# RWKV output product in a hybrid decoder trunk: group-norm statistics, powers, copies and weight splits in another order on VectorE, ScalarE and GpSimd

## The chip, the cores and the metric

The kernel runs on one core of one Trainium2 chip, in float32. The metric is the device time of one execution in microseconds (us). Before the change it is 726.13 us, the median of three runs (725.26 to 726.57). One execution was also recorded by the hardware profiler; every time below that is not a median comes from that record, counted from the start of its span.

## The reference

The program is a decoder trunk of two layers over 256 tokens of width 1024: layer 0 mixes tokens with native sparse attention, layer 1 with RWKV-7, each followed by a squared-ReLU MLP and residual adds. The change touches the end of the RWKV mixer: the states give `y`, which is normalised per head of 64 columns (group norm), gets a bonus, is gated, and goes through the output product into the residual `x`.

```python
    _, ys = lax.scan(step, jnp.zeros((B, H, N, N), f32), xs)
    y = jnp.moveaxis(ys, 0, 1)
    mu = jnp.mean(y, axis=-1, keepdims=True)
    var = jnp.mean(jnp.square(y - mu), axis=-1, keepdims=True)
    yn = ((y - mu) * lax.rsqrt(var + GN_EPS)).reshape(B, S, D) * ln_w + ln_b
    bonus = jnp.sum(rh * kh * r_k.astype(f32).reshape(H, N), axis=-1, keepdims=True) * vh
    y = yn + bonus.reshape(B, S, D)
    return (y.astype(h.dtype) * g) @ w_out, v_first
...
            x = x + y
        x = x + sq_relu_mlp(rms_norm(x, norm_mlp[i]), mlp_w1[i], mlp_w2[i])
```

## The kernel before

**Layout.** The 256 tokens are two tiles of 128 rows, `t = 0` and `t = 1`; a tile of `y` is worked on in two halves of 512 columns (8 heads), `i = 0` and `i = 1`. Names carry both: `rsd10` belongs to tile 1, half 0. The scan runs in four chunks of 64 tokens; chunks 0 and 1 make `y0`, chunks 2 and 3 make `y1`.

**Weights.** Each large weight comes in chunks of 128x1024 by DMA into `wst` (four buffers). ScalarE rounds it to `wh` (line 231), VectorE makes the rest `wl = wst - wh` (line 233, the *split*), and a product is three TensorE matmuls: `wh*h` (267), `wl*h` (268), `wh*l` (269). Below, `wl116` to `wl120` and `rowl` are the splits of six chunks of the output weight. The last two chunks (`row0`, `row1`) stay whole and are multiplied in float32 at line 357.

**Group norm**, `group_norm` at line 1311, for each half: eight `bn_stats` on VectorE (1320), seven small VectorE operations on 128x8 values (1322 to 1328), then on GpSimd a power `rsd = rsd^-0.5` (1329, here *pow*) and a product `nb` (1330). With `rsd` and `nb` ScalarE scales the eight heads (1338; for tile 0, half 1, VectorE does it at 1335). VectorE multiplies by `ln_w`, adds the bonus and gates (1340, 1341, 1342, 128x512 each). TensorE transposes the half into `yTp` (1346). ScalarE copies it out rounded as `yTh` (1349), VectorE makes the rest `yTl` (1350), and of the second half the last two blocks go out whole as `yTf` (1352).

**Output product**, `out_proj` at line 329: TensorE multiplies tile 0 by all chunks into `roa00` and `roa01` (24 three-fold matmuls in the two halves of the weight's columns, then the float32 ones), VectorE adds the result to `x` (378), and `after` transposes `x` for the MLP (`m1p`, 301) and splits it (304, 305). Then tile 1 follows. Between them stand the transposes of tile 1's halves.

**What sets the order.** Each engine runs its instructions strictly in the order of its queue. The queue is made by a scheduler at build time, from the order in which the code issues and from `tc.issue_after(...)`, which keeps an instruction behind another in that order. In `out_proj`, `hold` names instructions behind which the splits of the output weight are issued. At the end of `rwkv` (line 1396 on) the generators of the product and of the norm are advanced alternately. `final` (1414) loads the last norm's weights `gf` with a DMA on GpSimd's queue.

The two places that the change reorders inside `group_norm`:

```python
                    P.tensor_tensor(rsd, rsd, neg_half[:, 0:1].to_broadcast([128, 8]), op=ALU.pow)
                    P.tensor_tensor(nb, bs_, rsd, op=ALU.mult)
...
                    last["yTh"] = act(oh[i][:, :n, sl], p[:, :n], AF.Copy)
                    last["yTl"] = V.tensor_tensor(ol[i][:, :n, sl], p[:, :n], oh[i][:, :n, sl].bitcast(F32), op=ALU.subtract)
                    if i:
                        last["tail"] = act(of[:, :, sl], p[:, 2:], AF.Copy)
```

Of the kernel before, what the change touches and what calls it, by code (L numbers as in the profile page):

```python
# [9 lines left out]
F32 = mybir.dt.float32  # L10
F32R = mybir.dt.float32r
AF = mybir.ActivationFunctionType
ALU = mybir.AluOpType
# [3 lines left out]
D = 1024  # L17
# [5 lines left out]
DH = 64  # L23
# [3 lines left out]
GN_EPS = 64e-5  # L27
# [148 lines left out]
def trunk(ctx: ExitStack, tc: tile.TileContext, wb, x_in, wg, cw1k, cw1v, cw2, vecs_in, l1, w2, a2, g2, rows,  # L176
# [4 lines left out]
    V = nc.vector  # L181
# [103 lines left out]
    last_split, last_tr = [None, None], [None]  # L285

# [588 lines left out]
    def rwkv(inp):  # L875
        hn, dx, xrh, xrl, w2t, a2t, lo = inp
        with ExitStack() as es:
# [433 lines left out]
            def group_norm(t, y_):  # L1311

                for i in range(2):
                    cs = slice(512 * i, 512 * i + 512)
                    hs = slice(8 * i, 8 * i + 8)
                    bst, bs_, rsd, nb = [sm.tile([128, 8] + e, F32, tag=f"{n}", bufs=2, name=f"{n}{t}{i}")
                                         for n, e in (("bst", [6]), ("bs", []), ("rsd", []), ("nb", []))]
                    with tc.issue_after(st_done[1].ins) if t == 0 else ExitStack():
                        for h in range(8):
                            V.bn_stats(bst[:, h], y_[:, (8 * i + h) * DH:(8 * i + h + 1) * DH])  # L1320

                        V.tensor_tensor(nb, bst[:, :, 1], bst[:, :, 4], op=ALU.subtract)
                        V.tensor_tensor(rsd, bst[:, :, 2], bst[:, :, 5], op=ALU.add)
                        V.tensor_tensor(nb, nb, nb, op=ALU.mult)
                        V.tensor_tensor(bs_, bst[:, :, 1], bst[:, :, 4], op=ALU.add)
                        V.scalar_tensor_tensor(rsd, nb, DH / 4.0, rsd, op0=ALU.mult, op1=ALU.add)
                        V.tensor_scalar(bs_, bs_, -0.5, None, op0=ALU.mult)
                        last["stat"] = V.tensor_scalar(rsd, rsd, 1.0 / DH, GN_EPS, op0=ALU.mult, op1=ALU.add)
                    P.tensor_tensor(rsd, rsd, neg_half[:, 0:1].to_broadcast([128, 8]), op=ALU.pow)
                    P.tensor_tensor(nb, bs_, rsd, op=ALU.mult)  # L1330
# [19 lines left out]
                    last["yTl"] = V.tensor_tensor(ol[i][:, :n, sl], p[:, :n], oh[i][:, :n, sl].bitcast(F32), op=ALU.subtract)  # L1350
                    if i:
                        last["tail"] = act(of[:, :, sl], p[:, 2:], AF.Copy)
                    else:
                        last["head"] = last["yTh"], last["yTl"]
# [40 lines left out]
            hl, after = mlp_input(V_GM1, "m1")  # L1395
# [80 lines left out]
```

## Time and profile before

| what | value |
|---|---|
| median of three runs | 726.13 us (725.26 to 726.57) |
| the profiled execution | 725.32 us, of which its span is 723.4 us |
| TensorE (PE) busy | 704.7 us, 97% of the span |
| VectorE (DVE) busy | 466.1 us, 64% |
| ScalarE (ACT) busy | 437.0 us, 60% |
| GpSimd (POOL) busy | 20.9 us, 3% |
| the stretch that the change touches | about 490 to 535 us of the span |

A row of the timeline gives the start, the duration, engine, line, operation, what it writes and reads, how many instructions are merged, and in brackets the idle time of the engine before it with what ended it. Names stand there without buffer numbers. The queues of the engines overlap: a 128x512 VectorE operation is recorded for 0.69 us, while the next independent one starts after 0.60.

### The profile page before, as it was taken

The page shows a single profiled execution, that of the slowest core. Times are in us where ns is not written, and L with a number is a line of the kernel's source. Part 1 is how long each engine was busy: PE and PEld are TensorE (multiplying, and loading weights), DVE is VectorE, ACT ScalarE, POOL GpSimd, SP SyncE. Part 2 cuts the span into 40 slices and gives each one's busy share as a digit, 9 for nine tenths or more (in the row PEclk, how much of TensorE's full clock was granted, in tenths as well). Part 3 has the DMA queues.
Part 4 walks back from the last instruction along what each step waited for, and adds up shares of the span by engine and source line. Part 5 has one row for each costly group of instructions (what it writes and reads, how often), then busy time and mean ns, then how long its engine had stood idle before and what let it go on. Part 6 is the DMA issues. An engine that isn't in the chain of part 4 may idle for free.

```text
span 723.4 us, 13471 instructions
## 1 busy us (share of the span) xinstructions
PE 704.7 (97%) x5290; PEld 600.4 (83%) x5290; DVE 466.1 (64%) x1010; ACT 437.0 (60%) x882; POOL 20.9 (3%) x38
## 2 busy tenths in 40 slices
PE   9999999999999999999999999997999999999996
PEld 7877776789899989998889987686679889998894
DVE  5775899538645445456794879978756455454544
ACT  6735688328655555566275896766557555555552
POOL 1000000000000000000100010002300000000000
PEclk9999999999999999999999999999999999999998
DMA  7947020125755555578015432143428555555521
GB/s 286 318 168 292 25 93 2 59 88 207 235 180 195 180 181 196 177 228 268 1 59 175 137 109 63 31 148 102 163 78 267 183 196 181 188 189 177 195 95 58
DMA packets 32156, 111.64 MB, mean 154 GB/s; under 512 B 3677, under 2 KB 4189, under 8 KB 32094
## 3 DMA queue, kind: packets, MB, share of 16 engines
q1 hardware_dynamic: 31022, 109.08, 44.7%
q10 hardware_dynamic: 928, 1.19, 0.7%
q8 instruction: 41, 0.67, 0.4%
q0 software_dynamic: 144, 0.52, 0.2%
q14 instruction: 21, 0.17, 0.1%
HBM read 108.69 MB, written 1.05 MB: 152 GB/s over the span
## 4 chain that ended last, share of the span: by engine, by line
PE 83%; DVE 9%; ACT 4%; issue 2%; DMA 1%; SPq 0%; POOLq 0%; POOL 0%; DVEq 0%; ACTq 0%
PE mu L267 9%; PE mu L268 8%; PE mu L269 8%; PE mo L267 8%; PE mo L269 8%; PE mo L268 8%; PE acc L268 2%; PE acc L269 2%; PE acc L267 2%; PE S L654 2%; PE pa L268 2%; PE pa L267 2%; PE pa L269 2%; DVE pd L1201 2%; DVE Tb L1204 1%
## 5 line engine op out<-in xcount | busy, mean ns | idle before, releaser
L233 DVE TENSOR_TENSOR wl<-wst,wh 128x1024 fp32r<-128x1024 f32 x175 | 213.7, 1224 | 172.4 <-ACT wh L231 171.8
L231 ACT ACTIVATE wh<-wst 128x1024 fp32r<-128x1024 f32 x175 | 184.9, 1061 | 158.0 <-PE mu L268 77.5
L267 PE MATMUL mo<-wh,mqh 128*128 128x512 f32 x224 | 88.6, 397 | 0.0
L268 PE MATMUL mo<-wl,mqh 128*128 128x512 f32 x224 | 88.4, 395 | 0.0
L269 PE MATMUL mo<-wh,mql 128*128 128x512 f32 x224 | 87.4, 396 | 0.0
L267 PE MATMUL mu<-m0h,wh 128*128 128x256 f32 x256 | 72.5, 285 | 0.4 <-DVE m0l L305 0.4
L269 PE MATMUL mu<-m0h,wl 128*128 128x256 f32 x256 | 72.3, 283 | 0.0
L268 PE MATMUL mu<-m1l,wh 128*128 128x256 f32 x256 | 72.0, 282 | 0.0
L268 PE MATMUL mu<-m0l,wh 128*128 128x256 f32 x256 | 71.8, 282 | 0.0
L269 PE MATMUL mu<-m1h,wl 128*128 128x256 f32 x256 | 71.7, 281 | 0.0
L267 PE MATMUL mu<-m1h,wh 128*128 128x256 f32 x256 | 71.3, 282 | 0.0
L269 PEld LDWEIGHTS mo<-wh,mql 128*128 128x128 f32 x224 | 42.1, 188 | 10.3
L267 PEld LDWEIGHTS mu<-m0h,wh 128*128 128x128 f32 x256 | 48.2, 189 | 1.8 <-DVE m0l L305 0.6
L268 PEld LDWEIGHTS mu<-m0l,wh 128*128 128x128 f32 x256 | 48.4, 189 | 1.3 <-DVE m0l L305 0.2
L268 PEld LDWEIGHTS mu<-m1l,wh 128*128 128x128 f32 x256 | 48.2, 188 | 1.2
L267 PEld LDWEIGHTS mu<-m1h,wh 128*128 128x128 f32 x256 | 47.8, 188 | 1.2
L268 PEld LDWEIGHTS mo<-wl,mqh 128*128 128x128 f32 x224 | 42.2, 188 | 8.0
L267 PEld LDWEIGHTS mo<-wh,mqh 128*128 128x128 f32 x224 | 42.1, 188 | 7.7
L269 PEld LDWEIGHTS mu<-m1h,wl 128*128 128x128 f32 x256 | 48.2, 188 | 0.0
L269 PEld LDWEIGHTS mu<-m0h,wl 128*128 128x128 f32 x256 | 48.1, 188 | 0.0
L267 PE MATMUL acc<-wh,n0h 128*128 128x512 f32 x80 | 31.9, 405 | 0.1
L268 PE MATMUL acc<-wl,n0h 128*128 128x512 f32 x80 | 31.3, 397 | 0.2 <-DVE wl L233 0.2
(378 smaller groups left out, 1429.7 us busy)
## 6 DMA issues: line engine op xcount, KB each, us to landing
wst<-in_wb_dram SPq DMA_DIRECT2D x186, 512.0 KB, 4.1
w1t<-in_cw1k_dram SPq DMA_DIRECT2D x4, 512.0 KB, 6.1
w1t<-in_cw1v_dram SPq DMA_DIRECT2D x4, 512.0 KB, 7.0
x<-in_x_dram SPq DMA_DIRECT2D x4, 256.0 KB, 4.9
VS<-vt ACTq DMA_DIRECT2D x8, 128.0 KB, 4.6
row<-in_wb_dram SPq DMA_DIRECT2D x2, 512.0 KB, 4.7
out_dram<-xg SPq DMA_DIRECT2D x4, 256.0 KB, 2.1
g<-in_l_dram SPq DMA_DIRECT2D x2, 320.0 KB, 5.8
```

What stands on the lines that cost most here:

```text
L231: act(wh, st, AF.Copy)
L233: wl_done.append(V.tensor_tensor(wl, st, wh.bitcast(F32), op=ALU.subtract))
L267: mm(o, lh, rh, start=first, stop=False)
L268: mm(o, lh, rl, start=False, stop=False)
L269: return mm(o, ll, rh, start=False, stop=last)
L654: mm(S1, qT[gp][:, hg, 128:256], kT[gp][:, s], start=True, stop=True)
L1201: V.tensor_tensor(pd[:, a, :m_], Tb[:, a, i][:, :, None].to_broadcast(sh), Lb[:, i, n:][:, None, :].to_broadcast(sh), op=ALU.mult)
L1204: V.tensor_tensor(Tb[:, a, n:], Tb[:, a, n:], pd[:, a, :m_], op=ALU.add)
```

## The change

It sets the order of the norm's work by hand. The statistics of a half become a function, `gn_stats`, with their own places in the order: for tile 1, half 0, they come behind the `yTl` of tile 0, half 0; for tile 1, half 1, behind the split that is fourth in the output product (`wl119`). On GpSimd the product `nb` of one half comes ahead of the power of the next. `yTf` is copied ahead of `yTl`. The holds of the splits name other instructions, and the load of `gf` comes behind the last `nb`.

```diff
+            def gn_stats(t, i, y_):
+
+                bst, bs_, rsd, nb = [sm.tile([128, 8] + e, F32, tag=f"{n}", bufs=2, name=f"{n}{t}{i}")
+                                     for n, e in (("bst", [6]), ("bs", []), ("rsd", []), ("nb", []))]
+                with tc.issue_after((last["wl3"] if i else last["head"][1]) .ins if t else st_done[1].ins):
+                    for h in range(8):
+                        V.bn_stats(bst[:, h], y_[:, (8 * i + h) * DH:(8 * i + h + 1) * DH])
...
+                with tc.issue_after(last["nb"].ins) if i else ExitStack():
+                    P.tensor_tensor(rsd, rsd, neg_half[:, 0:1].to_broadcast([128, 8]), op=ALU.pow)
+                last["nb"] = pool_last[0] = P.tensor_tensor(nb, bs_, rsd, op=ALU.mult)
+                return rsd, nb
...
-                    last["yTl"] = V.tensor_tensor(ol[i][:, :n, sl], p[:, :n], oh[i][:, :n, sl].bitcast(F32), op=ALU.subtract)
                     if i:
                         last["tail"] = act(of[:, :, sl], p[:, 2:], AF.Copy)
-                    else:
+                    last["yTl"] = V.tensor_tensor(ol[i][:, :n, sl], p[:, :n], oh[i][:, :n, sl].bitcast(F32), op=ALU.subtract)
+                    if not i and not t:
                         last["head"] = last["yTh"], last["yTl"]
...
+            stat0 = last["stat"]
+            first_half = gn_stats(1, 0, y[1])
+            n_wl = len(wl_done)
             out = out_proj(lambda k, sl: kt(oh, k)[:, sl], lambda k, sl: kt(ol, k)[:, sl], "ro", after, tail=8, own=3,
-                           hold=[(last["stat"].ins, last["VS", 1].ins)] * 2 + [(last["o"].ins, last["VS", 3].ins)]
-                           + [[i_.ins for i_ in last["head"]] + [last["yc"].ins]], whole=of, marks=last)
+                           hold=[(stat0.ins, last["VS", 1].ins)] * 2 + [(last["head"][1].ins, last["VS", 3].ins)]
+                           + [[last["head"][0].ins, last["stat"].ins, last["yc"].ins]], whole=of, marks=last)
             next(out)
             done(AR, Wt)
             next(out)
-            norm = group_norm(1, y[1])
+            last["wl3"] = wl_done[n_wl + 3]
+            norm = group_norm(1, y[1], first_half)
...
-        P.dma_start(gf, bass.AP(tensor=rows.tensor, offset=rows.offset, ap=[[0, 128], [1, D]]))
+        with tc.issue_after(pool_last[0].ins):
+            P.dma_start(gf, bass.AP(tensor=rows.tensor, offset=rows.offset, ap=[[0, 128], [1, D]]))
```

The small statistics operations and the scaling loop are the same code as before, moved. Line numbers behind line 285 grow, by 2 in the helpers and by 7 to 12 in the places below.

GpSimd's queue, the four powers (`rsd` with `neg_half`) and products (`nb`), before, from the second power on:

```order
L1329 TENSOR_TENSOR rsd01_5750<-rsd01_5750,neg_half_71 128x8
L1330 TENSOR_TENSOR nb00_5676<-bs00_5674,rsd00_5675 128x8
L1330 TENSOR_TENSOR nb01_5751<-bs01_5749,rsd01_5750 128x8
L1329 TENSOR_TENSOR rsd10_5886<-rsd10_5886,neg_half_71 128x8
L1416 DMA gf_7819<-in_rows_dram 128x1024
L1330 TENSOR_TENSOR nb10_5887<-bs10_5885,rsd10_5886 128x8
L1329 TENSOR_TENSOR rsd11_5943<-rsd11_5943,neg_half_71 128x8
```

Now, from the first product on:

```order
L1330 TENSOR_TENSOR nb00_5676<-bs00_5674,rsd00_5675 128x8
L1329 TENSOR_TENSOR rsd01_5750<-rsd01_5750,neg_half_71 128x8
L1330 TENSOR_TENSOR nb01_5751<-bs01_5749,rsd01_5750 128x8
L1329 TENSOR_TENSOR rsd10_5794<-rsd10_5794,neg_half_71 128x8
L1330 TENSOR_TENSOR nb10_5795<-bs10_5793,rsd10_5794 128x8
L1329 TENSOR_TENSOR rsd11_5943<-rsd11_5943,neg_half_71 128x8
L1330 TENSOR_TENSOR nb11_5944<-bs11_5942,rsd11_5943 128x8
L1428 DMA gf_7819<-in_rows_dram 128x1024
```

`nb00` moved ahead of the power of `rsd01`, and the load of `gf` from between `rsd10` and `nb10` to the end.

VectorE's queue behind the last gating of `y0`, before:

```order
L233 TENSOR_TENSOR wl118_5822<-wst118_5818,wh118_5820 128x1024
L1320 BN_STATS bst10_5884<-y1_5636 128x6 x8
L1322 TENSOR_TENSOR nb10_5887<-bst10_5884 128x8
L1323 TENSOR_TENSOR rsd10_5886<-bst10_5884 128x8
L1325 TENSOR_TENSOR bs10_5885<-bst10_5884 128x8
L1324 TENSOR_TENSOR nb10_5887<-nb10_5887 128x8
L1327 TENSOR_SCALAR bs10_5885<-bs10_5885 128x8
L1350 TENSOR_TENSOR yTl0_5489<-yTp_5705,yTh0_5487 128x4x128
L1326 SCALAR_TENSOR_TENSOR rsd10_5886<-nb10_5887,rsd10_5886 128x8
L1328 TENSOR_SCALAR rsd10_5886<-rsd10_5886 128x8
L1320 BN_STATS bst11_5941<-y1_5636 128x6 x8
L1322 TENSOR_TENSOR nb11_5944<-bst11_5941 128x8
```

Now, from the same place:

```order
L1359 TENSOR_TENSOR yTl0_5489<-yTp_5705,yTh0_5487 128x4x128
L1319 BN_STATS bst10_5792<-y1_5636 128x6 x8
L233 TENSOR_TENSOR wl118_5843<-wst118_5839,wh118_5841 128x1024
L1321 TENSOR_TENSOR nb10_5795<-bst10_5792 128x8
L1322 TENSOR_TENSOR rsd10_5794<-bst10_5792 128x8
L1324 TENSOR_TENSOR bs10_5793<-bst10_5792 128x8
L1323 TENSOR_TENSOR nb10_5795<-nb10_5795 128x8
L1326 TENSOR_SCALAR bs10_5793<-bs10_5793 128x8
L1325 SCALAR_TENSOR_TENSOR rsd10_5794<-nb10_5795,rsd10_5794 128x8
L1327 TENSOR_SCALAR rsd10_5794<-rsd10_5794 128x8
L233 TENSOR_TENSOR wl119_5855<-wst119_5851,wh119_5853 128x1024
L1319 BN_STATS bst11_5941<-y1_5636 128x6 x8
```

`yTl0` moved to the front, and directly behind the last operation on `rsd10` stands a split, `wl119`, where before the eight statistics of the next half stood.

VectorE's queue further on, before:

```order
L233 TENSOR_TENSOR wl119_5834<-wst119_5830,wh119_5832 128x1024
L1323 TENSOR_TENSOR rsd11_5943<-bst11_5941 128x8
L1325 TENSOR_TENSOR bs11_5942<-bst11_5941 128x8
L1324 TENSOR_TENSOR nb11_5944<-nb11_5944 128x8
L233 TENSOR_TENSOR wl120_5846<-wst120_5842,wh120_5844 128x1024
L1327 TENSOR_SCALAR bs11_5942<-bs11_5942 128x8
L1326 SCALAR_TENSOR_TENSOR rsd11_5943<-nb11_5944,rsd11_5943 128x8
L233 TENSOR_TENSOR rowl_5858<-wst121_5854,rowh_5856 128x1024
L1350 TENSOR_TENSOR yTl1_5490<-yTp_5780,yTh1_5488 128x2x128
L1328 TENSOR_SCALAR rsd11_5943<-rsd11_5943 128x8
L1340 TENSOR_TENSOR y1_5636<-y1_5636,lnw_5365 128x512
```

Now, from the split of chunk 120 on:

```order
L233 TENSOR_TENSOR wl120_5867<-wst120_5863,wh120_5865 128x1024
L233 TENSOR_TENSOR rowl_5879<-wst121_5875,rowh_5877 128x1024
L1321 TENSOR_TENSOR nb11_5944<-bst11_5941 128x8
L1359 TENSOR_TENSOR yTl1_5490<-yTp_5780,yTh1_5488 128x2x128
L1322 TENSOR_TENSOR rsd11_5943<-bst11_5941 128x8
L1324 TENSOR_TENSOR bs11_5942<-bst11_5941 128x8
L1323 TENSOR_TENSOR nb11_5944<-nb11_5944 128x8
L1347 TENSOR_TENSOR y1_5636<-y1_5636,lnw_5365 128x512
L1326 TENSOR_SCALAR bs11_5942<-bs11_5942 128x8
L1325 SCALAR_TENSOR_TENSOR rsd11_5943<-nb11_5944,rsd11_5943 128x8
L1348 TENSOR_TENSOR y1_5636<-y1_5636,vt1_4609 128x512
L1327 TENSOR_SCALAR rsd11_5943<-rsd11_5943 128x8
```

The last operation on `rsd11`, which the fourth power reads, moved from ahead of the `ln_w` multiplication of tile 1, half 0, to behind that and behind the bonus addition (1348 now).

On TensorE one thing moves: the four `m1p` transposes of the second half of `x`'s columns, tile 0, from between the matmuls of tile 1 to directly behind those of the first half, ahead of the `yTp` transposes of tile 1, half 1.

## Rows read from the trace of the kernel before

**Rows 1.** From the page: its first line, and the shares of the chain that ended last.

```profile
span 723.4 us, 13471 instructions
...
PE 83%; DVE 9%; ACT 4%; issue 2%; DMA 1%; SPq 0%; POOLq 0%; POOL 0%; DVEq 0%; ACTq 0%
```

**Rows 2.** Timeline of TensorE: start, duration, line, out<-in, count, [idle before <- releaser].

```profile
495.82 0.68 PE L1261 MATMUL pZ<-W,AR 64*64 64x64 f32 x28
497.72 1.15 PE L1271 MATMUL pQ<-Zt,TT 64*64 64x64 f32 x32 [1.22 <-ACT Zt L1263]
...
501.63 0.66 PE L1346 MATMUL yTp<-cst,y 128*128 128x128 f32 x4 [0.26 <-DVE y L1342]
...
506.28 0.50 PE L267 MATMUL roa<-wh,yTh 128*128 128x512 f32 x1 [1.71 <-DVE yTl L1350]
...
512.91 0.40 PE L269 MATMUL roa<-wh,yTl 128*128 128x512 f32 x1
...
517.26 0.63 PE L1346 MATMUL yTp<-cst,y 128*128 128x128 f32 x4 [0.60 <-DVE y L1342]
...
520.87 0.63 PE L1346 MATMUL yTp<-cst,y 128*128 128x128 f32 x4 [0.82 <-DVE y L1342]
```

**Rows 3.** The chain that ended last, in order of time: the second `m1p` group.

```profile
525.93 0.44 PE m1p L301 x4
```

**Rows 4.** Timeline of GpSimd: powers (L1329) and products (L1330) of the norm.

```profile
491.93 2.36 POOL L1329 TENSOR_TENSOR rsd<-rsd,neg_half 128x8 f32<-128x8 f32 x1
494.26 0.20 POOL L1330 TENSOR_TENSOR nb<-bs,rsd 128x8 f32<-128x8 f32 x1
...
506.68 1.64 POOL L1329 TENSOR_TENSOR rsd<-rsd,neg_half 128x8 f32<-128x8 f32 x1 [11.79 <-ACT wh L231]
...
509.06 1.24 POOL L1330 TENSOR_TENSOR nb<-bs,rsd 128x8 f32<-128x8 f32 x1
...
513.77 0.20 POOL L1330 TENSOR_TENSOR nb<-bs,rsd 128x8 f32<-128x8 f32 x1
```

**Rows 5.** Timeline of VectorE: splits (L233), statistics, gating, last operation on `rsd11`.

```profile
491.56 2.35 DVE L233 TENSOR_TENSOR wl<-wst,wh 128x1024 fp32r<-128x1024 f32 x2
...
502.21 0.69 DVE L1342 TENSOR_TENSOR y<-y,g 128x512 f32<-128x512 f32 x1
...
506.41 1.11 DVE L1320 BATCH_NORM_STATS2 bst<-y 128x6 f32<-128x64 f32 x8
...
507.64 1.22 DVE L233 TENSOR_TENSOR wl<-wst,wh 128x1024 fp32r<-128x1024 f32 x1
...
509.03 1.21 DVE L233 TENSOR_TENSOR wl<-wst,wh 128x1024 fp32r<-128x1024 f32 x1
...
511.79 0.16 DVE L1328 TENSOR_SCALAR rsd<-rsd 128x8 f32<-128x8 f32 x1
```

**Rows 6.** Timeline of ScalarE: copies of the state, scalings (L1338), the copy of `yTf`.

```profile
491.99 1.59 ACT L1274 ACTIVATE VS<-pQ 64x256 f32<-64x256 f32 x4 [0.49 <-PE pQ L1271]
494.49 2.76 ACT L1338 ACTIVATE y<-y,nb,rsd 128x64 f32<-128x64 f32 x8 [0.91 <-POOL nb L1330]
...
511.91 0.39 ACT L1352 ACTIVATE yTf<-yTp 128x256 f32<-128x256 f32 x1 [4.12 <-DVE yTl L1350]
512.19 5.41 ACT L1338 ACTIVATE y<-y,nb,rsd 128x64 f32<-128x64 f32 x16
```

**Rows 7.** Stretches at the span's end: length, busy time of each engine, granted clock, DMA.

```profile
718.00:719.00 1.00, 0.00 (x0) 0.00 (x0) 0.33 (x2) 0.17 (x1) 0.56 (x1) 1.00 0.00 0
719.00:720.00 1.00, 0.00 (x0) 0.00 (x0) 0.31 (x1) 0.55 (x1) 0.00 (x0) 0.55 0.00 0
```

**Rows 8.** Timeline of TensorE: its last matmul.

```profile
715.91 0.40 PE L269 MATMUL mo<-twh,mql 128*128 128x512 f32 x1
```

**Rows 9.** Timeline of TensorE at the span's start, the warm-up matmuls.

```profile
1.05 3.79 PE L477 MATMUL warmp<-warmz 128*128 128x128 f32 x16 [1.05 <-DVE warmz L472]
...
6.11 1.50 PE L477 MATMUL warmp<-warmz 128*128 128x128 f32 x12
```

More of the change, by code (lines that the diff above doesn't have):

```diff
@@ L285, in trunk @@
     last_split, last_tr = [None, None], [None]
+    pool_last = [None]
     def after_split():
@@ L1309, in output @@
                     done(Ms[c], VS[c])
-            def group_norm(t, y_):
+            def gn_stats(t, i, y_):
[4 more added lines that the diff above has]
+                        V.bn_stats(bst[:, h], y_[:, (8 * i + h) * DH:(8 * i + h + 1) * DH])
+                    V.tensor_tensor(nb, bst[:, :, 1], bst[:, :, 4], op=ALU.subtract)
+                    V.tensor_tensor(rsd, bst[:, :, 2], bst[:, :, 5], op=ALU.add)
+                    V.tensor_tensor(nb, nb, nb, op=ALU.mult)
+                    V.tensor_tensor(bs_, bst[:, :, 1], bst[:, :, 4], op=ALU.add)
+                    V.scalar_tensor_tensor(rsd, nb, DH / 4.0, rsd, op0=ALU.mult, op1=ALU.add)
+                    V.tensor_scalar(bs_, bs_, -0.5, None, op0=ALU.mult)
+                    last["stat"] = V.tensor_scalar(rsd, rsd, 1.0 / DH, GN_EPS, op0=ALU.mult, op1=ALU.add)
+                with tc.issue_after(last["nb"].ins) if i else ExitStack():
+                    P.tensor_tensor(rsd, rsd, neg_half[:, 0:1].to_broadcast([128, 8]), op=ALU.pow)
+                last["nb"] = pool_last[0] = P.tensor_tensor(nb, bs_, rsd, op=ALU.mult)
+                return rsd, nb
@@ L1313, in group_norm @@
+            def group_norm(t, y_, first_half=None):
                 for i in range(2):
                     cs = slice(512 * i, 512 * i + 512)
[L1315 to L1328, printed above, removed]
@@ L1329, in group_norm @@
-                    P.tensor_tensor(rsd, rsd, neg_half[:, 0:1].to_broadcast([128, 8]), op=ALU.pow)
-                    P.tensor_tensor(nb, bs_, rsd, op=ALU.mult)
+                    rsd, nb = first_half if first_half and not i else gn_stats(t, i, y_)
                     with tc.issue_after(st_done[2].ins) if t == 0 and i else ExitStack():
```

## The prediction, made before the changed kernel ran

> **What bounds the kernel now.** I read the page first: of the chain that ended last, 83% is TensorE's, so time is saved or lost only where TensorE waits, or where it is given other work [rows 1]. Then TensorE's timeline between 490 and 535, for its waits: 1.22 us until `Zt` is copied, 0.26 for the first `yTp`, 1.71 until VectorE has made `yTl0`, 0.60 and 0.82 for the gated halves of `y1` [rows 2]. They sum to 4.6 us, 0.6% of the span, and no order can give back more. Last come the engines that are waited for: VectorE's queue [rows 5], ScalarE's scalings [rows 6], and GpSimd's powers [rows 4], which look idle (3% busy) but stand in the middle of each norm.
>
> **The change part by part.** Times are on the scale of the profiled execution. Terms 2 to 4 are worked out as if all ahead of 502 stayed where it is; term 1 then moves the whole of it.
>
> *Term 1, `nb00` ahead of the second power.* Now `nb00` starts at 494.26, after the second power (491.93, 2.36 us), and ScalarE idles 0.91 us for it before the first scalings [rows 4, 6]. Changed, `nb00` is issued at 492.0, when the first power ends. It then stands beside the two splits of 491.56 [rows 5]. What a GpSimd operation does that starts inside a split is in the rows: `nb10` started at 509.06, 0.03 after a split, and lasted 1.24 us, to 0.06 after the split's end, where `nb11`, beside nothing, took 0.20; and the second power, started inside the first of the two splits, lasted 0.7 longer than the third (1.64) and came through between the two [rows 4, 5]. So it is held until the split in progress ends. `nb00` ends at 492.8, ScalarE is free at 491.99 + 1.59 = 493.6, the scalings run 493.6 to 496.35 instead of 494.49 to 497.25 [rows 6]. TensorE has `pZ` done at 496.50, so `Zt` and `pQ` come 0.7 earlier and VectorE's gating of `y0` 0.9 earlier; the first `yTp`, which had 0.26 of waiting on top, moves from 501.63 by 0.9 [rows 2]. Were `nb00` held over both splits (to 494.0), it would be 0.5. I take **-0.9**, since the row next to it slipped through.
>
> *Term 2, `yTl0` first.* VectorE ends its gating at 502.9 [rows 5]. Now 118's split and the statistics come before `yTl0`, and TensorE waits 1.71. Changed: `yTl0` 502.95; eight statistics 503.55 (1.11 recorded, the next may start after 1.03); `wl118` 504.6 (1.14 from start to start: two take 2.35); seven small operations from 505.7 to 506.5; `wl119` 506.45; eight statistics 507.6; `wl120` 508.6; `rowl` 509.75; one small; `yTl1` 511.0 to 511.4. TensorE starts the product 1.7 earlier, and meets `rowl` and `yTl1` at its 28th and 29th matmul. The 29th, now at 512.91, goes at 511.45: of 1.7 us 1.45 is left. From there to the next `yTp` is 517.26 - 512.91 - 0.60 = 3.75 us of work, so that could stand at 515.2 instead of 517.26 [rows 2].
>
> *Term 3, powers behind splits.* This is where the change pays. Before, the power of `rsd10` started at 506.68 beside the statistics and took 1.64 unhindered [rows 4, 5]. Changed, `wl119` follows `rsd10` at once, so the power starts 0.2 after a split has begun: held to 507.55, done 509.2. `nb10` then starts inside `wl120` and ends with it, at 509.9. ScalarE, no longer stopped 4.12 us by `yTf` behind `yTl1` [rows 6], waits for this instead: eight scalings of 0.34, 509.95 to 512.65. VectorE, there at 511.57, multiplies by `ln_w` from 512.7, adds at 513.5, and only then does the last operation on `rsd11`, 514.1 to 514.3, that ended at 511.95 before [rows 5]. The fourth power starts inside the gating of 514.25 to 514.95, is done at 516.45, `nb11` at 516.7 (before: 513.97 [rows 4]), the scalings at 519.45, where they ended at 512.19 + 5.41 = 517.60 [rows 6]. The five VectorE operations from there to the second gating are the same in number and sum, so the second `yTp` of tile 1, at 520.87 now, comes at 522.7: **+1.8**. The gain of term 2 runs out here: it only makes TensorE wait longer. The gating of 514.95 is still in time for the `yTp` of 515.2.
>
> *Term 4, `m1p`.* The second group of four transposes took 0.44 us between tile 1's matmuls [rows 3]; now it fills a wait: **-0.45**.
>
> *Costed at nothing.* `gf` is needed only in the last MLP, 170 us later. The DMA that refills 118's buffer goes out 1.7 later than at 504, for a rounding behind 522. The new semaphore waits of ScalarE's scalings are for statistics long done.
>
> The sum is -0.9 + 1.8 - 0.45 = **+0.45 us**.
>
> *Term 5, TensorE's clock.* TensorE's first `m1p` group ends at 515.2 + (520.87 - 0.82 - 517.26) = 518.0, and the next work, for which VectorE adds to `x` behind the delayed scalings, starts at 522.05: one wait of 4.1 us in place of several short ones. In the whole trace TensorE's longest wait between its first and last matmul is the 1.71 of [rows 2], with the granted clock at 1.00. Behind its last matmul, over at 716.3 [rows 8], the clock is 1.00 until 719 and then falls to half, 1.2 GHz: the mean of 0.55 puts the fall at 719.1, 2.8 us later [rows 7]. A wait of 4.1 us lies beyond that, so I expect the lower level when tile 1's matmuls begin. What it costs no row shows in mid-run. Below it is nothing, if the clock recovers at once. Above: the first 16 warm-up matmuls took 0.237 us each, those at 6.11 0.125 [rows 9]; half speed from 1.05 to about 6 loses 2.4 us. I take the middle, **+1.2**, since the end of the low stretch may fall anywhere.
>
> The Trainium skill, "TensorE: Matmul & The Clock Gate", section "HAM oscillation — how this bites in real kernels", tells of a kernel whose waits for data let the clock fall to half, so that each next burst of matmuls starts slow; by that rule the wait speaks against this change. The fall after the last matmul agrees [rows 7]; that a wait in mid-run does it, no row here shows.
>
> The Trainium skill, "SBUF — State Buffer", section "Who interferes with whom", says that the engine that comes first, GpSimd or a VectorE operation with two inputs in SBUF, holds the shared ports for its whole instruction. The half that holds GpSimd agrees with [rows 4, 5]. The other half does not: the split of 507.64 began inside the power of 506.68 to 508.32 and took its usual 1.22 [rows 5]. By the rule the split of 508.6 would wait for the power's end at 509.2; the rival below has what follows.
>
> **The rivals.**
> 1. *GpSimd is held, the clock stays up.* 726.13 + 0.45 = 726.6. For it: how long a wait the chip bears in mid-run is not in the trace, and where the fall came may have been late. This is the nearest case on the other side.
> 2. *GpSimd isn't held.* Then the third power runs 506.65 to 508.3, `nb10` is ready at 508.5, VectorE goes on at 511.57 without waiting, `rsd11` is ready 1.1 earlier, the fourth power ends at 514.95, the scalings at 517.9, 0.3 later than before. Sum 0.3 - 0.45 - 0.9 = -1.05: 725.1, the most that I see in the change. Against it: every power or product that began beside a split in [rows 4] was stretched.
> 3. *GpSimd is held longer.* `nb10` doesn't come through between `wl120` and `rowl`, which stand back to back, and ends with `rowl` at 511.05: 1.1 more, 726.13 + 0.45 + 1.1 + 1.2 = 728.9. It decides from a gap that is too short; the second power found one.
> 4. *A power in progress stops a split.* `wl120` at 509.2 makes `nb10` 0.5 later: 0.95 + 1.2, 728.3. The row above speaks against it.
>
> That the change doesn't do what it says isn't open: the queues stand as built.
>
> **How the numbers follow.** The profiled execution took 725.32, 0.8 below the median; the terms are differences, and I add them to the median. Forecast (held, clock falls): 726.13 + 0.45 + 1.2 = **727.8**, chance 0.45, by itself 726.6 to 729.0 for a price of the clock of 0 to 2.4. Rival 1 0.25, rival 2 0.17, rivals 3 and 4 0.08 together, anything else 0.05. About 0.2%, 1.45 us, is what a measurement of this kernel can tell from no change: slower is above 727.6, faster below 724.7. In the forecast the price decides: above 1.0 of 0 to 2.4 it is slower, 0.26 of its 0.45; with rivals 3 and 4 and some of the rest 0.36. Rival 1 and the other part of the forecast and most of rival 2 are the same: 0.55. Faster is the lower end of rival 2 and some of the rest: 0.09. The range of 8 in 10 takes in rivals 1 to 4 with half a microsecond below rival 2: 724.6 to 729.2.
>
> **What would show it.** Right: the first scalings start 0.9 earlier and TensorE's wait for `pQ` shrinks to about 0.5; no wait ahead of the first `roa` matmul; the power of `rsd10` lasts about 2.5 us and `nb10` about 0.6; VectorE idles over 1 us ahead of tile 1's first `ln_w`; TensorE has one wait of about 4 us ahead of the second `m1p`; and behind it a stretch with a granted clock below 1.00 and matmuls of twice the length. Wrong: a third power of 1.64 us beside `wl119` (term 3 falls, rival 2), or the 4 us wait at a clock that stays at 1.00 (term 5 falls, rival 1).

## The result, and the profile after

The changed kernel took 730.41 us (median of five runs, 728.52 to 731.5), the kernel before 725.54 beside it (724.5 to 726.57): a ratio of 1.0056, with a 95% interval of 1.0038 to 1.0075. The middle of the forecast was 1.7 us slower, though the prediction gave 0.55 to no measurable change and 0.36 to slower. It is slower, by 4.9 us, and outside of the range.

The profiled execution of the changed kernel has a span of 728.5 us, 5.1 more than [rows 1]. Since the two executions differ ahead of the change too, I measure by a stretch that holds only the change and the work behind it: from the start of GpSimd's first power to the start of the last matmul. Before: 715.91 - 490.31 = 225.60 us [rows 8]. After: 720.36 - 491.16 = 229.20. So 3.60 of the 5.1 us lie there; 0.85 came ahead of it, and 0.65 behind the last matmul.

TensorE's timeline of the changed kernel (start, duration, line, out<-in, count, [idle before <- releaser]):

```profile
497.87 1.15 PE L1273 MATMUL pQ<-Zt,TT 64*64 64x64 f32 x32 [0.53 <-ACT Zt L1265]
...
504.29 0.48 PE L267 MATMUL roa<-wh,yTh 128*128 128x512 f32 x1
...
516.12 0.63 PE L1353 MATMUL yTp<-cst,y 128*128 128x128 f32 x4 [0.88 <-DVE y L1349]
516.59 1.88 PE L359 MATMUL roa<-row,yTf 128*128 128x512 f32 x4
518.31 0.60 PE L303 MATMUL m1p<-cst,x 128*128 128x128 f32 x4
523.12 1.11 PE L303 MATMUL m1p<-cst,x 128*128 128x128 f32 x4 [4.21 <-DVE x L380]
...
526.59 0.63 PE L268 MATMUL roa<-wl,yTh 128*128 128x512 f32 x1
527.02 0.63 PE L269 MATMUL roa<-wh,yTl 128*128 128x512 f32 x1
...
528.12 0.39 PE L269 MATMUL roa<-wh,yTl 128*128 128x512 f32 x1
528.35 0.40 PE L267 MATMUL roa<-wh,yTh 128*128 128x512 f32 x1
```

Of the waits of [rows 2], the one for `Zt` is 0.53 instead of 1.22, the one ahead of the first `roa` matmul is gone, and the one for the gated first half of `y1` is 0.88 instead of 0.60. A new one of 4.21 us stands ahead of the second `m1p` group, for VectorE's addition to `x`. Behind it a matmul follows the one before after 0.43 us; from 528 on it is 0.23 again. The granted clock of the same stretch (length, busy time of PE, PEld, DVE, ACT and POOL, granted clock, DMA):

```profile
520.00:521.00 1.00, 0.00 (x0) 0.00 (x0) 0.42 (x1) 1.00 (x4) 0.00 (x0) 1.00 1.04 377
521.00:522.00 1.00, 0.00 (x0) 0.00 (x0) 1.00 (x3) 0.28 (x2) 0.00 (x0) 0.52 0.25 86
...
526.00:527.00 1.00, 1.00 (x3) 0.73 (x3) 0.76 (x3) 0.30 (x2) 0.00 (x0) 0.50 0.00 0
527.00:528.00 1.00, 1.00 (x4) 0.78 (x3) 0.00 (x0) 0.31 (x1) 0.00 (x0) 0.57 0.00 0
528.00:529.00 1.00, 1.00 (x6) 0.81 (x5) 0.22 (x1) 1.00 (x3) 0.00 (x0) 1.00 0.00 0
```

The clock falls to half (1.2 GHz) at 521.0, 2.1 us after TensorE's last work, and comes back at 527.9, 4.7 us after the next work began. (In the second profile of this kernel, below, it falls at 521.4 and comes back at 528.2: 2.5 us and 5.1 us.) Where the 4.21 us come from, GpSimd shows (`nb00`, the second power, the third, `nb10`, the fourth, `nb11`):

```profile
492.88 0.80 POOL L1330 TENSOR_TENSOR nb<-bs,rsd 128x8 f32<-128x8 f32 x1
493.65 2.62 POOL L1329 TENSOR_TENSOR rsd<-rsd,neg_half 128x8 f32<-128x8 f32 x1
...
506.62 2.48 POOL L1329 TENSOR_TENSOR rsd<-rsd,neg_half 128x8 f32<-128x8 f32 x1 [9.96 <-ACT wh L231]
509.19 1.79 POOL L1330 TENSOR_TENSOR nb<-bs,rsd 128x8 f32<-128x8 f32 x1
515.41 2.06 POOL L1329 TENSOR_TENSOR rsd<-rsd,neg_half 128x8 f32<-128x8 f32 x1 [4.44 <-DVE rsd L1327]
517.55 0.20 POOL L1330 TENSOR_TENSOR nb<-bs,rsd 128x8 f32<-128x8 f32 x1
```

and VectorE beside it (`wl119`, `wl120`, `rowl`, the first `ln_w` of tile 1, the last operation on `rsd11`, the second `ln_w`, the second addition to `x`):

```profile
506.39 1.23 DVE L233 TENSOR_TENSOR wl<-wst,wh 128x1024 fp32r<-128x1024 f32 x1
...
508.55 1.21 DVE L233 TENSOR_TENSOR wl<-wst,wh 128x1024 fp32r<-128x1024 f32 x1
509.68 1.22 DVE L233 TENSOR_TENSOR rowl<-wst,rowh 128x1024 fp32r<-128x1024 f32 x1
...
513.81 0.69 DVE L1347 TENSOR_TENSOR y<-y,lnw 128x512 f32<-128x512 f32 x1 [2.23 <-ACT y L1345]
...
515.17 0.17 DVE L1327 TENSOR_SCALAR rsd<-rsd 128x8 f32<-128x8 f32 x1
...
520.58 0.69 DVE L1347 TENSOR_TENSOR y<-y,lnw 128x512 f32<-128x512 f32 x1 [4.00 <-ACT y L1345]
...
522.39 0.68 DVE L380 TENSOR_TENSOR x<-x,roa 128x512 f32<-128x512 f32 x1
```

and ScalarE with tile 1's scalings, which wait for `nb10` and for `nb11`:

```profile
511.01 2.77 ACT L1345 ACTIVATE y<-y,nb,rsd 128x64 f32<-128x64 f32 x8 [2.99 <-POOL nb L1330]
517.78 2.76 ACT L1345 ACTIVATE y<-y,nb,rsd 128x64 f32<-128x64 f32 x8 [4.01 <-POOL nb L1330]
```

Read together: the third power stretched by `wl119`, `nb10` held not to the end of `wl120` (509.76) but to that of `rowl` (510.90); the scalings of half 0 therefore late, VectorE waiting 2.23 us; the last operation on `rsd11`, queued behind, at 515.17 instead of 511.79 [rows 5]; the fourth power behind it; and a wait of 4.00 us on VectorE, which passes on to TensorE. VectorE's queue has a part in that last step: the matmuls that the second addition to `x` reads end at 518.47 (516.59 + 1.88), but the addition stands behind the `ln_w` multiplication that waits, and comes at 522.39. No run here puts it ahead of that multiplication.

### The profile page after: what moved, and what is told of

Same layout as the page of the kernel before. It is cut to its first block, busy times and chain, and to the rows that moved or that the text cites. A ratio compares the mean times of both kernels' runs of the same rounds, so it can differ in the third digit from the quotient of the medians.

```text
span 728.5 us, 13474 instructions
## 1 busy us (share of the span) xinstructions
PE 707.1 (97%) x5290; PEld 602.1 (83%) x5290; DVE 465.5 (64%) x1010; ACT 436.6 (60%) x882; POOL 23.5 (3%) x38
## 4 chain that ended last, share of the span: by engine, by line
PE 83%; DVE 9%; ACT 4%; issue 2%; DMA 1%; POOL 0%; SPq 0%; POOLq 0%; DVEq 0%
PE mu L267 8%; PE mu L268 8%; PE mu L269 8%; PE mo L267 8%; PE mo L269 8%; PE mo L268 8%; PE acc L268 2%; PE acc L269 2%; PE acc L267 2%; PE S L656 2%; PE pa L268 2%; PE pa L267 2%; PE pa L269 2%; DVE pd L1203 2%; DVE Tb L1206 1%
## 5 line engine op out<-in xcount | busy, mean ns | idle before, releaser
L233 DVE TENSOR_TENSOR wl<-wst,wh 128x1024 fp32r<-128x1024 f32 x175 | 213.6, 1224 | 173.7 <-ACT wh L231 173.1
```

The source lines that it names most:

```text
L233: wl_done.append(V.tensor_tensor(wl, st, wh.bitcast(F32), op=ALU.subtract))
```

## The experiments

In this table "stretch" is the one from the first power's start to the last matmul, of the profiled execution; the ratio is to the kernel before in the same set of runs.

| kernel | stretch, us | ratio (95%) |
|---|---|---|
| before; again | 225.60; 225.67 | 1 |
| changed; again | 229.20; 229.37 | 1.0056 (1.0038 to 1.0075); 1.0067 (1.0050 to 1.0084) |
| before, `nb00` ahead | 224.70 | 0.9995 (0.9984 to 1.0007) |
| changed, 28 needless matmuls | 228.94 | 1.0048 (1.0034 to 1.0063) |
| changed, 16 needless matmuls | 227.35 | 1.0050 (1.0034 to 1.0066) |
| changed, `rsd11` ahead of `ln_w` | 223.59 | 0.9976 (0.9963 to 0.9989) |
| changed, `rsd11` ahead of `ln_w`, `nb10` on VectorE | 223.69 | 0.9980 (0.9964 to 0.9996) |
| changed, statistics ahead of `wl119` | 222.76 | 0.9948 (0.9931 to 0.9966) |
| changed, `rowl` last | 223.65 | 0.9983 (0.9971 to 0.9995) |
| changed, `wl119` in the statistics | 222.31 | 0.9954 (0.9935 to 0.9973) |

**The two kernels again.** The changed kernel a second time:

> The changed kernel once more, beside the kernel before on the same chip. Its profile began the norm's stretch 0.85 us later than the kernel before (TensorE waited 1.35 instead of 0.81 us at 471 and 0.63 instead of 0.36 at 477), at code that the change does not touch. Theory A, that this belongs to one execution: the two waits come back at other lengths, and the ratio is 1.004 to 1.007 all the same. Rival, that it belongs to the changed program: 1.35 and 0.63 come back to 0.05 us. In both cases the product of GpSimd for tile 1, half 0, should again last about 1.8 us, if being held through two splits is not chance.

The kernel before a second time:

> The kernel before, profiled a second time, for the stretch ahead of the norm, in which five profiles of changed kernels began the first power at 490.7 to 491.6 us, and the profile of the kernel before at 490.3. Theory A, TensorE's waits at 471 and 477 us (0.81 and 0.36 us in the kernel before, 1.15 to 1.35 and under 0.2 to 0.91 in the others) have lengths of chance, which belong to one execution: here they differ from 0.81 and 0.36 too, by up to 1 us in the start of the first power. Rival, they belong to the changed program: 0.81, 0.36 and 490.3 come back to 0.1 us.

In the changed kernel every row of the norm came back, `nb10` with 1.80 us and TensorE's wait with 4.21. The rows ahead of it came back too, or nearly: waits of 1.25 and 0.63 us (1.35 and 0.63 in the first profile), the first power at 491.18 (491.16). By that run alone, the rival would stand. The kernel before, though, began its first power at 492.59 this time, 2.28 us later than in its first execution, with a longer wait of TensorE and a clock that fell to half in the middle of the scan. Its rows, from TensorE's timeline, then those of the first execution:

```profile
471.93 1.15 PE L1257 MATMUL pZ<-VS,M 128*64 128x64 f32 x32 [1.83 <-DVE TT L1232]
473.01 1.94 PE L1183 MATMUL pKB<-cst,BK 128*128 128x128 f32 x8
```

```profile
470.57 1.15 PE L1257 MATMUL pZ<-VS,M 128*64 128x64 f32 x32 [0.81 <-DVE TT L1232]
471.65 1.09 PE L1183 MATMUL pKB<-cst,BK 128*128 128x128 f32 x8
```

The second row took 1.09 us there, where the clock stayed up. So the start of the norm moves by more than 0.85 us between two executions of one kernel; and in the six profiles of the changed kernel and its variants in which the clock did not fall ahead of the norm, it lies between 490.71 and 491.61. The 0.85 us are no more than such differences; that no part of them belongs to the change is not shown.

**Term 1 alone.** Kernel before, with

```diff
-                    P.tensor_tensor(rsd, rsd, neg_half[:, 0:1].to_broadcast([128, 8]), op=ALU.pow)
-                    P.tensor_tensor(nb, bs_, rsd, op=ALU.mult)
+                    with tc.issue_after(last["nb"].ins) if t == 0 and i else ExitStack():
+                        P.tensor_tensor(rsd, rsd, neg_half[:, 0:1].to_broadcast([128, 8]), op=ALU.pow)
+                    last["nb"] = P.tensor_tensor(nb, bs_, rsd, op=ALU.mult)
```

> The kernel before with one part of the change: the product nb00 ahead of the second power on GpSimd's queue, nothing else. Theory A, term 1 of the prediction by itself: nb00 lasts 0.8 us and ends with the first split, the scalings follow ScalarE's copies without their 0.91 us of waiting, and 0.9 us come off: ratio to the kernel before 0.9988. Rival, nothing of it is left at the first tile-1 matmul, since the order behind it (the split of 118 and the statistics ahead of yTl0) sets the time: the wait ahead of the first roa matmul grows from 1.71 to 2.6, ratio 1.000.

`nb00` lasted 0.80 us again, and the stretch is 0.90 to 0.97 shorter. The wait ahead of the first `roa` matmul stays at 1.70, so the rival, by which it would grow to 2.6, falls. The timing, -0.05% with an interval of -0.16 to +0.07%, holds both 0.9 us and nothing; the stretch decides.

**What the clock costs.** In the changed kernel, ahead of tile 0's second `m1p` group,

```diff
+            if (name, t, cbs) == ("m1", 0, (1,)):
+                for j in range(28):
+                    mm(p[:, j % 4], ident, ident, start=True, stop=True)
```

> The changed kernel with 28 needless 128x128 matmuls between the two m1p groups of tile 0, which fill TensorE's wait of 4.2 us (28 x 0.125 = 3.5 us at full clock) and are overwritten. Nothing else moves ahead of the wait. Theory A, the wait costs twice, once as waiting and once as clock: the granted clock stays at 1.00 between 519 and 530, the first seven threefold matmuls of tile 1 start 0.23 us apart instead of 0.43, and the kernel is 2.2 us faster than the changed one, ratio to the kernel before about 1.003 (728.0 where the changed one has 730.2). Rival, the lower clock is only a bystander and the matmuls are slow for their operands: no gain, ratio 1.006.

Here my sizing was off: the trace has two instructions for each of these matmuls, and the 56 took 6.42 us, so that the second `m1p` group started 1.9 us later than in the changed kernel, counted from the first power. The clock stayed at 1.00, and the stretch is 0.26 us shorter all the same; the ratio, 1.0048, can't be told from the changed kernel's. The same with `range(16)`:

> The changed kernel with 16 needless matmuls in TensorE's wait in place of the 28 of the run before, in which each was two instructions and the 56 took 6.42 us, 1.9 us longer than the wait. 16 take 3.7 us and fit into it. Theory A, the clock has a price of 2.2 us by itself: the granted clock stays 1.00, the second m1p group starts where it did in the changed kernel, counted from the first, the next matmuls start 0.23 us apart, ratio to the kernel before 1.003 (changed: 1.0056 and 1.0067). Rival, a shorter wait than in the changed kernel is what the run before gained by: no gain, 1.006.

TensorE's timeline in this kernel:

```profile
523.83 0.66 PE L306 MATMUL m1p<-cst,x 128*128 128x128 f32 x4 [0.64 <-DVE x L383]
...
525.22 0.39 PE L268 MATMUL roa<-wl,yTh 128*128 128x512 f32 x1
525.45 0.39 PE L269 MATMUL roa<-wh,yTl 128*128 128x512 f32 x1
```

The second group starts 31.96 us after the first power, as in the changed kernel (523.12 - 491.16 = 31.96), so nothing moved ahead of it, and behind it the clock is what differs, 1.00 here. The stretch is 1.85 us shorter than in the changed kernel's first profile, and 2.02 than in its second, where the clock came back 0.4 us later. That is the price of the clock by these three profiles: 1.9, not the expected 2.2. The timing (1.0050, where 1.003 was expected) cannot confirm it; its interval holds the changed kernel's ratio as well.

**The late `rsd11`.** Changed kernel; the statistics of half 1 are issued from within the product, with no other place, and

```diff
...
-                    with tc.issue_after((wl_done[-1] if t else st_done[2]).ins):
+                    with tc.issue_after((wl_done[-1] if t else st_done[2]).ins), tc.issue_after(last["stat"].ins) if t else ExitStack():
                         V.tensor_tensor(y_[:, cs], y_[:, cs], lnw[0][:, cs], op=ALU.mult)
...
```

> The changed kernel with one group moved on VectorE: the last three operations on bs11 and rsd11 stand ahead of the ln_w multiplication of tile 1, half 0, as in the kernel before. Theory A, the late rsd11 is what turns a short hold into a long wait: the fourth power starts at 511.9 and runs beside nothing (1.64 us), the second half's scalings follow the first half's without a gap (513.8 to 516.5 instead of 517.8 to 520.5), TensorE's wait ahead of the second m1p shrinks from 4.2 to about 0.5 us, the clock stays at 1.00, and of the 4.9 us lost 6.4 come back: 0.997 of the kernel before. Rival, GpSimd's hold of the third power and product (506.6 to 511.0) is what costs, whatever follows: the wait stays above 2 us, and the ratio above 1.002.

GpSimd's fourth power and product, then TensorE:

```profile
511.61 1.64 POOL L1332 TENSOR_TENSOR rsd<-rsd,neg_half 128x8 f32<-128x8 f32 x1 [1.08 <-DVE rsd L1330]
513.33 0.20 POOL L1333 TENSOR_TENSOR nb<-bs,rsd 128x8 f32<-128x8 f32 x1
```

```profile
518.91 0.66 PE L303 MATMUL m1p<-cst,x 128*128 128x128 f32 x4 [0.45 <-DVE x L383]
```

All as theory A had it: the power beside nothing, a wait of 0.45 us, the clock at 1.00, 5.6 us off the stretch, 0.9976 where 0.997 was expected. Three small operations, 0.5 us of VectorE's time, decided whether the changed order loses 0.6% or gains 0.24%. In this kernel the third power (2.48) and `nb10` (1.79) are held just as long; by themselves, then, the holds don't cost what was lost.

**`nb10` on VectorE**: the changed kernel without GpSimd's `nb10`, with `rowl` held behind VectorE's. In VectorE's queue the last operation on `rsd11` stands ahead of `ln_w` here too.

```diff
...
+                with tc.issue_after(wl_done[-1].ins):
+                    last["nb"] = V.tensor_tensor(nb, bs_, rsd, op=ALU.mult)
...
```

> As the run before it (rsd11 ahead of ln_w again), and the product nb10 is made by VectorE between the splits wl120 and rowl, where GpSimd's was held to 510.98. Theory A: the scalings of tile 1, half 0, start at 510.0 instead of 511.0, but the second half still waits for the fourth power (513.6), so that nothing is left of it at TensorE's second m1p: within 0.6 us of the run before, ratio 0.996 to 0.998. Rival, the hold of the product is on the path by itself: 1.0 us better than the run before, 0.9955 or less.

223.69 us against 223.59, and 0.9980 against 0.9976: nothing is left, as theory A said. The wait of 0.89 us that the run on `rsd11` has ahead of the `yTp` of tile 1's first half is gone, and the one ahead of the second `m1p` grew to 1.69 (the clock stayed up): the second half still waits for its power.

**Three splits in a row behind all statistics.** Changed kernel, `gn_stats(1, 1)` issued behind `wl118`, and

```diff
...
+                return [last["stat"].ins] if n >= 3 else ()
...
```

as a further hold of `wl119` and the splits behind it.

> The changed kernel with all of the statistics of tile 1, half 1 (the eight bn_stats and the seven small operations), moved ahead of wl119, so that the three splits wl119, wl120 and rowl stand in a row behind them. The third power then starts beside bn_stats and takes 1.64 us; nb10 arrives 0.05 us into wl119, the fourth power behind it. Theory A, a GpSimd operation comes through at the end of a split if it came early into it: nb10 ends with wl119, the scalings of half 0 start at 509.5 (on the scale of the changed kernel), the fourth power comes through behind wl120, and TensorE's long wait is gone with the clock's fall: from the start of the first power to the last matmul 221.8 us, where the kernel before has 225.6 and the changed one 229.2; ratio to the kernel before about 0.995. Rival, GpSimd is held over the whole row, as it was over wl120 and rowl: scalings from 511.7, 223.2 us, ratio 0.997. TensorE waits up to 0.7 us for wl119 in both.

GpSimd (the third power, `nb10`, the fourth power) and VectorE (`wl119` and `wl120`, then `rowl`):

```profile
507.04 1.64 POOL L1332 TENSOR_TENSOR rsd<-rsd,neg_half 128x8 f32<-128x8 f32 x1 [9.96 <-DVE bst L1322]
508.76 1.20 POOL L1333 TENSOR_TENSOR nb<-bs,rsd 128x8 f32<-128x8 f32 x1
509.92 2.61 POOL L1332 TENSOR_TENSOR rsd<-rsd,neg_half 128x8 f32<-128x8 f32 x1
```

```profile
508.68 2.37 DVE L233 TENSOR_TENSOR wl<-wst,wh 128x1024 fp32r<-128x1024 f32 x2
510.96 1.22 DVE L233 TENSOR_TENSOR rowl<-wst,rowh 128x1024 fp32r<-128x1024 f32 x1
```

`nb10` came through at the end of `wl119`, the power at the end of `wl120`: theory A, with TensorE's longest wait in the product 0.58 us. 222.76 us where 221.8 was expected, and 0.9948: the fastest of the set by its median, 722.85 us against 726.40. The gain in the stretch fell 1 us short of its estimate; some of that is VectorE's operations on `y1`, which I had follow each other after 0.60 us, and which do after 0.73.

**`rowl` behind the small operations.** Changed kernel, `gn_stats(1, 1)` issued behind `wl119` as in the run on `rsd11`, `rowl` held behind its last operation.

> The changed kernel with the split rowl moved behind the seven small operations of tile 1, half 1, and so with a gap between wl120 and rowl. Theory A: nb10 (2.48 us of power ahead of it, as before) ends with wl120 at 509.8 instead of 510.98, the scalings of half 0 start 1.15 us earlier, rsd11 is done at 510.8, and its power is held by rowl until 512 and done at 513.5; second-half scalings 513.9 to 516.6 instead of 517.8 to 520.5; no wait over 1.5 us on TensorE, clock 1.00; 223.2 us from the first power to the last matmul, ratio 0.997. Rival, rowl, 1.15 us later, is what TensorE waits for now: a wait of over 1 us ahead of rowl's matmul at 511.5, ratio 0.999 or more.

```profile
510.35 0.67 POOL L1333 TENSOR_TENSOR nb<-bs,rsd 128x8 f32<-128x8 f32 x1
512.10 2.54 POOL L1332 TENSOR_TENSOR rsd<-rsd,neg_half 128x8 f32<-128x8 f32 x1 [1.09 <-DVE rsd L1330]
```

With other operations between the two splits `nb10` takes 0.67 us, and ends with `wl120`; the power, beside `rowl`, 2.54. TensorE's longest wait is 1.01 us, for `x`, none for `rowl`. 223.65 us (expected 223.2), 0.9983 (expected 0.997).

**`wl119` between statistics and small operations.** In the last variant the statistics of tile 1, half 1, are issued in two parts; `wl119` comes behind the eight `bn_stats`, and `wl120` and `rowl` behind the small operations. The part for `wl119`:

```diff
...
+                if n == 3:
...
+                    next(second)
+                    return [last["bn"].ins]
...
```

> As the run with all statistics of the second half ahead of wl119 (0.9948 of the kernel before), but with wl119 between the eight bn_stats and the seven small operations. Theory A: TensorE's wait of 0.58 us for wl119 goes, nb10, which came 0.08 us into wl119 and lasted 1.20, comes to its end 0.8 us earlier, the fourth power is held by wl120 as it was, and the second half's scalings start 0.1 us behind its nb11; 222.2 us from the first power to the last matmul instead of 222.8, and a ratio of 0.994. Rival, the operations behind wl119 hold nb10 further (wl119 stands 0.13 us behind a bn_stats, as wl120 did in the changed kernel, and the next operation starts 1.125 us behind it), and the first half's scalings start later than in that run: 223 us or more, 0.996.

`nb10` took 0.37 us, the wait for `wl119` is gone, and 0.64 us of waiting for `rowl` came instead: 222.31 us, 0.9954. By the stretch it is 0.45 us better than the run with three splits in a row, by the ratio not to be told from it.

**When GpSimd comes through.** Products without use, 51 in the kernel before and 40 in the changed one:

> The kernel before with 51 needless products of 128x8 on GpSimd between 466 and 490 us, where it is idle, beside VectorE's 128x1024 operations with two inputs in SBUF: two from 466.7, one or two from 471.8, four back to back from 478.1. Theory A, an operation with two inputs in SBUF holds GpSimd, and whether a product comes through between two of them hangs on the gap: back to back, none to four products come through in 478 to 483, each other one lasting to an operation's end, and products beside copies out of PSUM take their 0.1 to 0.2 us. Rival, a product always comes through at an operation's end, and the product held through two splits was an exception: three products within the four operations. Second question: whether VectorE's operations are longer than 1.22 us beside GpSimd's; theory A says no.

> The changed kernel with 40 needless products of 128x8 on GpSimd between nb01 and the power of rsd10, so that one is always under way from 497 to past 511 us, and the power far later than in the changed kernel (the time is slower by some us and says nothing). Looked for: in the first of the pair wl120 and rowl a product stands that began within 0.3 us of the split's start. In the run with products beside four operations in a row one came through at each end, the next operation having started 1.14 us after the one before; wl120 and rowl start 1.125 us apart. Theory A, the gap decides: the product that began in wl120 lasts until rowl's end. Rival, the time at which the product comes decides (nb10 came 0.63 us into wl120, the others 0.1 to 0.5 us into theirs): the product comes through at wl120's end.

In the first, four of VectorE's 128x1024 operations stand in a row (two in each row of its timeline). The products of 480.25 to 484.7 are one group (count, busy, mean ns, idle before):

```profile
480.18 2.35 DVE L1155 TENSOR_TENSOR M<-M,cst 128x1024 f32<-128x1024 f32 x2
482.46 2.35 DVE L1373 TENSOR_TENSOR vt<-vt,lnb 128x1024 f32<-128x1024 f32 x2
```

```profile
L1214 POOL TENSOR_TENSOR probe<-probe 128x8 f32<-128x8 f32 x4 | 4.4, 1110 | 0.3
```

Four operations, four products: one comes through at the end of each. That is what the rival says, though it counted three; theory A, which allowed for none to four, is not refuted by it. VectorE's operations kept their usual length beside them (two in 2.35 us), and so did `rowl` beside the fourth power in the run with three splits in a row (1.22), which also speaks against rival 4 of the prediction. In the second run VectorE's and GpSimd's rows are

```profile
509.87 1.21 DVE L233 TENSOR_TENSOR wl<-wst,wh 128x1024 fp32r<-128x1024 f32 x1
510.99 1.22 DVE L233 TENSOR_TENSOR rowl<-wst,rowh 128x1024 fp32r<-128x1024 f32 x1
```

```profile
500.78 2.66 POOL L1332 TENSOR_TENSOR probe<-neg_half 128x8 f32<-128x8 f32 x1
...
509.90 2.39 POOL L1332 TENSOR_TENSOR probe<-neg_half 128x8 f32<-128x8 f32 x1
```

The product that came 0.03 us into `wl120` was held through `rowl` as `nb10` had been, which came 0.63 into it. So it is not the time of coming that decides. The spacing of VectorE's operations goes with it. `rowl` starts 1.125 us after `wl120` in both kernels. In the row of four the next operation starts 1.132 to 1.143 us after the one before, in the run with three splits in a row 1.143 and 1.144. (These are the trace's starts in ns; the rounded rows can't tell them apart.) The same two splits, `wl120` and `rowl`, hold GpSimd over both at 1.125 and let it through at 1.144. The row of 500.78 says the same of shorter operations: it was held over four of 128x512 that start 0.60 apart, and came out where the next one started 0.71 later.

That the spacing goes with it is shown in these places, for the splits by a difference of 7 to 19 ns. Whether it is the cause isn't shown, and another difference goes along with it: in every profile in which GpSimd was held over `wl120` and `rowl`, `wl120` starts right behind a `bn_stats`, and no pair of 128x1024 operations that let GpSimd through does. Nor does a spacing of 1.124 hold GpSimd if a small operation follows: with `rowl` behind the small operations `wl120` was followed by one 1.124 later, and `nb10` ended 0.09 us behind `wl120`.

## Why the prediction was wrong

**Term 1 was right.** -0.9 forecast, -0.90 to -0.97 measured alone. `nb00` came through between two splits, as taken.

**Term 2 was right.** No wait ahead of the first `roa` matmul; `yTl0` at 502.90 and the operations behind it within 0.1 us of the listed times up to `yTl1`.

**Term 3 failed in one step**: "`nb10` then starts inside `wl120` and ends with it, at 509.9." The third power was held as forecast (2.48 for about 2.5), but `nb10` ended at 510.98. I had seen GpSimd come through between two splits and took it for the rule; those two start 1.14 us apart, these 1.125, and VectorE's 2.35 for two splits [rows 5] was the spacing that I used for both. Which feature of the second pair shuts GpSimd out stays open, as said above. All that follows was right in its order and late by the same 1.1 us: scalings of half 0 at 511.01 (forecast 509.95), `rsd11` at 515.17 (514.1), `nb11` done at 517.75 (516.7), scalings of half 1 done at 520.54 (519.45), second `m1p` at 523.12 (522.05). This was rival 3, with a chance of 0.08 together with rival 4. The Trainium skill, "SBUF — State Buffer", section "Who interferes with whom", has a VectorE instruction with two SBUF inputs contend with a GpSimd instruction that reads SBUF, over an exclusive lock. These runs agree that GpSimd waits to such an instruction's end (powers of 2.48 us, `nb00` of 0.80), and show a wait over two and four instructions besides (1.79 and 2.39, 2.66).

**Term 4** was not tried by itself. Terms 3 and 4 together: 227.35 (clock kept up) - 225.60 + 0.9 = +2.65 where +1.35 was forecast; 1.1 of the 1.3 are `nb10`'s, 0.2 stays open.

**Term 5: the mechanism was right, the size too small.** One wait of 4.1 us was forecast, 4.21 came; the clock fell. I took the middle of 0 and 2.4, since no row showed a fall in mid-run; it cost 1.85 to 2.02, near the upper end. The half clock lasted over all of the two transpose groups and seven matmuls, and I had no reason to expect less than the 5 us of the span's start [rows 9]: with an upper end from a row and a lower one from nothing, the row's side was the better choice. The Trainium skill, "TensorE: Matmul & The Clock Gate", section "HAM oscillation — how this bites in real kernels", has a kernel whose waits for data lower the clock for the work that follows. The trace agrees: behind the wait of 4.21 us the granted clock was 0.50.

**Not foreseen: 0.65 us at the end.** From the last matmul's start to the end of the span the changed kernel takes 8.14 us, the kernel before 7.49. The engines' rows are alike; the last transfers differ, in the changed kernel's DMA issues of the last 5.5 us (KB, median us to landing), which are 2.1 us before:

```profile
out_dram<-xg SPq DMA_DIRECT2D x2, 256.0 KB, 3.2
```

It goes with the program: 7.44 to 7.49 in the four profiles of the kernel before and its variants and 7.20 and 7.44 in the variants with `nb10` on VectorE and with `rowl` last, 8.08 to 8.17 in those of the changed kernel and the other variants. Only the kernel before and the changed kernel were profiled twice; for the others this rests on one profile each. Why the transfers differ isn't settled.

**The sum.** -0.9 + 2.9 (term 3 with 1.1 more) - 0.45 + 1.9 + 0.65 = +4.1 us, where the runs show 4.9 with an interval of 2.8 to 5.4. The range ended at 729.2, since I had put each of the two bad ends (`nb10` held longer; the clock's full price) beside the middle of the other. Both came. The costly edit was seen, the last operation on `rsd11` behind two that wait, but as one step in a chain, with no price of its own; the run that undoes it alone shows that without it the rest of the change gains 0.24%.

## What to carry to other kernels

A small operation that feeds another engine belongs ahead of anything in its queue that may wait: with three operations of 0.16 us each behind a waiting multiplication, VectorE's next wait was 4.00 us, and with them ahead of it 0.23; the long one passed on to TensorE and brought a lower clock. Reckon with GpSimd being shut out while VectorE runs operations with two SBUF inputs in close order, over several of them if need be. Put its small steps beside `bn_stats` (a power of 1.64 us) or VectorE's work out of PSUM (products of 0.20 us in the first run with products), where they take their usual time. Two costs that meet in one mechanism (a longer hold, a longer wait, a lower clock) should be given their bad ends together.

## What the runs showed of the hardware

The clock falls in the kernel before too, in some executions: to half at 473.1 in its second profile (back at 476.5), where TensorE had waited 1.83 us, and not in its first, where it had waited 0.81. Where it fell between 471 and 475 us, in five profiles, TensorE had just waited 1.15 to 1.83 us; in the two of the changed kernel it had waited 1.35 and 1.25 there, and the clock stayed up. In the run with only `nb00` moved it also fell at 427, behind 3.0 us of small matmuls (128x2 and 64x64, from 423.4 to 426.4), with TensorE busy for 96% and more of each us; in the first profile of the kernel before the clock stayed at 1.00 behind the same matmuls. The run's stretches:

```profile
425.00:426.00 1.00, 0.96 (x23) 0.81 (x21) 0.98 (x1) 0.97 (x4) 0.00 (x0) 1.00 0.54 139
426.00:427.00 1.00, 1.00 (x11) 0.89 (x11) 1.00 (x3) 0.94 (x4) 0.00 (x0) 0.97 0.86 332
427.00:428.00 1.00, 1.00 (x4) 0.81 (x3) 1.00 (x4) 0.96 (x4) 0.00 (x0) 0.50 0.86 131
```

Such falls outside the norm came in 7 of the 14 profiles. The first power starts at 490.31 to 491.61 us in the seven without one, at 491.87 to 492.59 in the six with one ahead of it, and at 494.13 in the one with two. By the means of the first two groups, 491.04 and 492.30, a fall goes with a start some 1.3 us later, which is an estimate, since the waits differ as well; a part of the runs' spread of 2 us may be theirs. The wait of 4.2 us lowered the clock in both profiles of the changed kernel.
